# Side transfers behind weight loads, and lighter side work, in a hybrid encoder layer

## The chip, the cores and the metric

The kernel runs on one core of a Trainium2 chip. The time is the device time of one execution in microseconds (us), from runs of the whole kernel; a profile is one execution recorded by the hardware profiler. TensorE (PE) multiplies, VectorE (DVE), ScalarE (ACT) and GpSimd (POOL) do elementwise work, and SyncE (SP) sends nearly every transfer of this kernel.

## The reference

One layer of a bidirectional encoder on 1280 token rows of 2048 features: 1024 of a sample sequence and 256 of a prompt sequence.

```python
hn = rms_norm(x, norm_g)
xbc, z_ssd, dt_raw, q, k, v, z_att, mq, z_mem = split_cols(hn @ w_in, IN_SIZES)
xbc = silu(centred_dwconv(xbc, conv_w, conv_b))          # 1536 columns, 5 taps
xs, Bm, Cm = split_cols(xbc, (1024, 256, 256))
y = ssd_scan(forward) + ssd_scan(backward) + d_skip * xs  # 16 heads of 64, chunks of 128
o_ssd = rms_norm(y * silu(z_ssd), ssd_norm_g)            # in two groups
o_att = window_attention(q, k, v, sink) * silu(z_att)    # 8 heads, window 128
mk, mv = split_cols(rms_norm(mem, mem_norm_g) @ w_mem_kv, (512, 512))
o_mem = softmax(mq . mk) mv * silu(z_mem)                # 4 heads over 256 memory rows
return x + concat(o_ssd, o_att, o_mem) @ w_out
```

All of it is in float32.

## The kernel before, in words

**Products.** Each float32 operand is split into a high part (h, H) and a low part (l, L), and three TensorE products stand for one. A weight tile `wraw` (128 x 512) comes by a transfer, ScalarE makes `wh` of it (L211), VectorE `wl` (L212): that is `wsplit`. Its two instructions are kept in `marks`.

The tokens are two groups of 640 rows. `block_tok` is a plain block: sixteen weight tiles, and for each of them five token tiles (four for the memory rows) with three matmuls each, 512 or 288 columns (L266 to L268). Its last two weight tiles are used together, so that one token tile after another is finished and read out (`evac`). `block_pair` is the other kind, a seven-product (Strassen) form: 256 output columns are a unit, a unit has eight weight tiles with 21 matmuls of 320 columns each (L1155 to L1157), and for each weight tile GpSimd makes sums `ws` (L1127) that ScalarE and VectorE split into `sh` and `sl` as well. `weight_sums` sends the load of a pair weight tile two steps ahead (`lead=2`).

**Stages, in order of time.** Two memory blocks (`mk`, `mv`); the q block of the first group; the first pair stage, ten units of the first group; the kv and mq blocks of the first group; the second pair stage, ten units of the second group; then a mixed stage of plain blocks (kv, q, mq, z0, z1 of the second group, z0, z1 of the first, and the output blocks) between whose weight steps attention, memory attention and the scan are run; last eight output pair units.

**Side work of the first stages.** `x_stats` squares rows of x in pieces of 512 columns on ScalarE, to get a row factor in `rx`; `x_rows(grp)` turns five such factors into a row vector `rbc` over the group's 640 tokens with small TensorE products and copies on VectorE (L1461, L1462). `scale_row` multiplies a row tile of the turned x (`x_turned`, 128 features by 640 tokens) by the gain and `rbc` (L1186). For the first group `p_first` loads such a row pair, `p_fill` scales and splits it into the resident tiles `xH`, `xL`, `p_sums` and `p_split` make the pair sums. For the second group the rows are scaled in the first pair stage: `first_side` squares rows 5 to 9 in pieces of 320 columns (`square_tasks`), runs `x_rows(1)`, then loads, scales and stores each of sixteen rows in two halves to `xs_d` in DRAM (`row_tasks`, 32 tasks). In the kv and mq blocks `t_step` follows a plan `t_plan`: `p_next` loads a row pair from `xs_d`, `p_sums` and `p_split` make the pair sums from it in place, and later `r_load` and `r_fill` load the row again and make `xH` and `xL` of it. `keep_x` stores the first group's `xH` and `xL` to DRAM, 16 transfers of 640 KB, since the first group comes back late in the mixed stage.

The side steps are taken by `pairs_in`: after each weight step of a unit it calls `next(side)` zero to two times (eight times a unit).

**Order.** The program is written in one order, and a scheduler makes each engine's queue of it, taking what is ready first by its own reckoning. `tc.issue_after(ins)` queues what is traced in its block behind `ins`, and it does so for instructions of the same engine as `ins` only. `behind()` and `step()` open it for the two instructions in `marks` (ScalarE and VectorE). `block_tok` has a parameter `spaced`, which opens it around `wsplit` for a matmul two weight tiles back.

**Lanes.** In the mixed stage two lanes hold generators: lane 0 the windowed and the memory attention (`k_prep`, `attn`, `mem_attn`), lane 1 the scan (`ssd_up`, `ssd_down`). Each `yield` ends a step. After each weight step `pump(rates)` runs so many steps of each lane as `RATES` says for the block. So a yield between two operations puts TensorE's weight products between them.

Of the kernel before, what the change touches and what calls it, by code (L numbers as in the profile page):

```python
# [21 lines left out]
KT = D // P  # L22
# [6 lines left out]
CH, WB, RB, WA, WBB = 4, 3, 4, 5, 4  # L29
RBB = 3  # L30

RATES = {'kv': (1.8, 2.4), 'q': (2.95, 3.25), 'mq': (2.95, 3.25), 'z1': (2.95, 3.25), 'z0': (2.95, 3.25), 'oa': (2.4, 4.5), 'o': (4.2, 3.4)}
FAR = 1e30
# [8 lines left out]
def hymba_encoder_kernel(  # L42
# [139 lines left out]
    def fill_direct(q, j, src, gain=None, n=640, norm=False):  # L182
# [24 lines left out]
    count, middle = [0], {}  # L207

# [6 lines left out]
    def w_laid(src, n):  # L215

        def load(k, raw):
            S.dma_start(raw, src[k])
        return load, n
# [18 lines left out]

    def block_tok(w, nt, evac, before_last=None, feats=range(KT), places=range(KT), spaced=False):

# [4 lines left out]
        for k in range(last + 1):  # L245
            raw = wp.tile([P, 512], F32, tag="wraw", name="wraw", bufs=RB)
            load(feats[k], raw[:, :n])
            with tc.high_priority(offset=HP[2]):
                h = wp.tile([P, 512], F32R, tag="wh", name="wh", bufs=WB)
                l = wp.tile([P, 512], F32R, tag="wl", name="wl", bufs=WB)  # L250
                with tc.issue_after(middle[count[0] - 2]) if spaced and count[0] - 2 in middle else ExitStack():
                    wsplit(raw[:, :n], h[:, :n], l[:, :n])
            count[0] += 1
            hls[k] = h, l
            if k == last - 1:
                continue
            if k == last and before_last is not None:
                before_last(k)

            for t in range(nt):  # L260
                for k_ in ((k - 1, k) if k == last else (k,)):
                    q, m = divmod(places[k_], 4)
                    h, l = hls[k_]
                    sh = cur["H", q][:, m, t * P:(t + 1) * P]
                    sl = cur["L", q][:, m, t * P:(t + 1) * P]
                    T.matmul(ps[t][:, :n], sh, h[:, :n], start=(k_ == 0), stop=False)  # L266
                    T.matmul(ps[t][:, :n], sh, l[:, :n], start=False, stop=False)  # L267
                    mm = T.matmul(ps[t][:, :n], sl, h[:, :n], start=False, stop=(k_ == last))  # L268
                if k < last and t == nt // 2:
                    middle[count[0] - 1] = mm.ins  # L270
                elif k == last and t in (1, 3):
                    middle[count[0] - 2 + t // 2] = mm.ins
# [158 lines left out]
    def k_prep(t):  # L431
# [20 lines left out]
        yield  # L452
        yield
        ps = psum("pk")
        kf = kh.rearrange("p a b d -> p (a b d)")
# [93 lines left out]
    def attn(t):  # L549
# [24 lines left out]
        for b in range(2):  # L574
# [3 lines left out]
            V.tensor_sub(qh[:, :, 1, :], qb, qh[:, :, 0, :].bitcast(F32))  # L578
            yield
            ps = psum("pq")  # L580
            qf = qh.rearrange("p a b d -> p (a b d)")
# [81 lines left out]
    def mem_attn(t):  # L663
# [77 lines left out]
        yield  # L741
        yield
        turn_(0)
        yield
        turn_(1)
        yield
        values(0)
# [9 lines left out]
    def ssd_up(t):  # L757
# [63 lines left out]
        for g in range(2):  # L821
# [14 lines left out]
            if not last:  # L836
                fl = wb("fl", F32R)
                V.tensor_sub(fl, xf, fh.bitcast(F32))
            if not first:
                xb = wb("xb")  # L840
# [269 lines left out]
    def weight_sums(src, i):  # L1110
# [7 lines left out]
        else:  # L1118
            raw = wp.tile([P, 512], F32, tag="wraw", name="wraw", bufs=RB)
        S.dma_start(raw, src[i // 8, i % 8])  # L1120
        with tc.high_priority(offset=HP[2]):
# [109 lines left out]
    def p_next(k):  # L1231
        p_load(k, lambda r: xs_d[r])

# [19 lines left out]
    for k in range(8):  # L1253
        at = (4, 7, 10, 13, 15, 17, 19, 21)[k]
        for j, f in ((at - 3, p_next), (at, p_sums), (at + 2, p_split)):
            t_plan.setdefault(j, []).append((f, k))
    for k, at in enumerate((25, 26, 27, 28, 29, 31, 33, 35)):
        for j, f in ((at - 2, r_load), (at, r_fill)):
            t_plan.setdefault(j, []).append((f, k))

    def t_step(j):
        with ExitStack() as st:
            for ins in marks:
                st.enter_context(tc.issue_after(ins))
            if j in (27, 29):
                weight_sums(w_in_pairs, (j - 27) // 2)
            for f, k in sorted(t_plan.get(j, ()), key=lambda x: ((p_split, r_fill, p_sums, p_next, r_load).index(x[0]), x[1])):
                f(k)
# [271 lines left out]
    for _ in first[0]():  # L1540
# [8 lines left out]

    run(block_tok(w_in_rows("q"), 5, ev_raw(q_d, 0), feats=PAIRED, places=PAIRED), (0, 0),  # L1550
        extra=lambda k: p_step(16 + k))
# [6 lines left out]
    def pairs_in(grp, extra, side):  # L1558
        nonlocal owe
        for u, unit in enumerate(units):  # L1560
            for k in block_pair(w_in_pairs, u, rows_in, ev_seven(*unit, grp), lead=2):
                for _ in range((0 if k == 7 else 2 if k in (1, 4) else 1) if grp == 0 else k in (0, 1, 2, 4, 5)):
                    next(side, None)
# [6 lines left out]
                if u == 0:  # L1570
                    extra(32 + k)
                elif grp == 0 and keep and k in (1, 3, 5):
                    keep_x(*keep.pop(0))

    side = first_side()
    pairs_in(0, p_step, side)
# [42 lines left out]
    def tok(name, i, evac, after=None, extra=None, hold=0):  # L1619
        run(block_tok(w_in_rows(name), 5, evac, spaced=True), RATES[name], after, extra=extra, hold=hold)  # L1620

# [56 lines left out]
    for c, part_ in ((0, 0), (1, 0), (0, 1), (1, 1)):  # L1678
        h = halves[part_]
        run(block_tok(w_out_rows(c), 5, ev_out(c, part_), feats=h, places=h, spaced=True), RATES["o" if part_ else "oa"], hold=-1,  # L1680
            extra=late_rows(c, part_))
    for c in (2, 3):
        j0 = 16 * c - 48
        for k in block_tok(w_out_rows(c), 5, ev_out(c), before_last=lambda _: beside_step(j0 + 14), spaced=j0 < -16):
            if j0 + k == -7:
# [89 lines left out]
```

## Time and profile before

| what | value |
|---|---|
| median of 3 runs | 1830.43 us (1821.97 to 1832.84) |
| the profiled execution | 1830.21 us, its span 1828.5 us |
| mean granted TensorE clock | 0.995 |
| instructions | 31223, of which 10306 matmuls |
| TensorE busy | 1780.6 us (97%) |
| VectorE, ScalarE, GpSimd busy | 1332.2 (73%), 952.7 (52%), 682.1 (37%) |
| HBM read and written | 255.53 MB and 76.61 MB, 182 GB/s over the span |

A row of the table of stretches gives the stretch and its length, then for each engine its busy us and in brackets its instructions, then the granted TensorE clock as a share of full speed, the mean busy share of the sixteen DMA engines, and GB/s. A row of groups gives the source line, engine, operation, output and inputs, shapes and count, then busy us and mean ns of one, then the idle time just ahead of them and what ended it. A row of the timeline gives start and length in us, engine, line and operation, and in square brackets the idle time ahead of it. A row of waits gives who waited for whom, us in total, times, and the longest. A row of transfers ends with KB each and the median us from issue to landing. Matmuls overlap, so a count of them over a stretch says more of the pace than their durations. PE is TensorE's matmuls, PEld its weight loads.

### The profile page before, as it was taken

How to read it: one execution, taken by the hardware profiler on the slowest of the kernel's cores; microseconds unless marked ns; L12 is line 12 of the kernel's file. 1: busy time of each engine (PE TensorE's matmuls, PEld its weight loads, DVE VectorE, ACT ScalarE, POOL GpSimd, SP SyncE). 2: the span in 40 equal slices, each digit the busy share in tenths (PEclk: the TensorE clock that was granted, in tenths of full speed). 3: DMA queues.
4: the chain of work that ended last, by engine and by line, in shares of the span. 5: the costliest groups of instructions: out<-in, count | busy, mean ns of one | idle time of the engine just before them, and what ended most of it. 6: DMA issues, size and time to landing. Idle time of an engine off the chain costs nothing.

```text
span 1828.5 us, 31223 instructions
## 1 busy us (share of the span) xinstructions
PE 1780.6 (97%) x10306; PEld 1573.9 (86%) x10306; DVE 1332.2 (73%) x2489; ACT 952.7 (52%) x2135; POOL 682.1 (37%) x1092
## 2 busy tenths in 40 slices
PE   9999999999999999999999999999999999999999
PEld 7788998889799999987778877887777787889999
DVE  5594787997867889886667767767787865666665
ACT  6554553333555544366567447656556744443332
POOL 0115787871068899511001110001111100048775
PEclk9999999999999999999999999999999999999999
DMA  8685554665754443374545577657688765644442
GB/s 292 206 314 198 153 153 142 188 190 150 255 171 123 143 119 109 99 216 131 178 133 152 170 237 262 209 175 215 221 282 256 241 207 155 204 152 145 144 135 85
DMA packets 224674, 334.21 MB, mean 183 GB/s; under 512 B 23104, under 2 KB 102144, under 8 KB 224512
## 3 DMA queue, kind: packets, MB, share of 16 engines
q1 hardware_dynamic: 224368, 332.17, 58.8%
q8 instruction: 81, 1.33, 0.3%
q14 instruction: 81, 0.66, 0.1%
q10 hardware_dynamic: 144, 0.06, 0.0%
HBM read 255.53 MB, written 76.61 MB: 182 GB/s over the span
## 4 chain that ended last, share of the span: by engine, by line
PE 64%; DMA 12%; issue 7%; DVE 7%; POOL 6%; ACT 3%; SPq 1%; POOLq 0%; DVEq 0%; ACTq 0%
PE acc L266 8%; PE acc L267 8%; PE acc L268 7%; PE acc L1157 7%; PE acc L1155 7%; PE acc L1156 7%; POOL ws L1127 3%; PE accm L1155 3%; PE accm L1156 3%; PE accm L1157 3%; PE py L887 2%; DMA wraw<-in_w_in_pairs_dram 1%; DVE wl L212 1%; POOL wraw L1127 1%; PE pmo L733 1%
## 5 line engine op out<-in xcount | busy, mean ns | idle before, releaser
L266 PE MATMUL acc<-wh,xH 128*128 128x512 f32 (+1 forms) x1248 | 483.7, 388 | 2.7 <-ACT wh L211 1.7
L267 PE MATMUL acc<-wl,xH 128*128 128x512 f32 (+1 forms) x1248 | 478.3, 383 | 4.2 <-DVE wl L212 4.1
L268 PE MATMUL acc<-wh,xL 128*128 128x512 f32 (+1 forms) x1248 | 475.5, 381 | 0.0
L212 DVE TENSOR_TENSOR wl<-wraw,wh 128x512 fp32r<-128x512 f32 (+1 forms) x480 | 350.9, 734 | 152.2 <-ACT wh L211 149.0
L211 ACT ACTIVATE wh<-wraw 128x512 fp32r<-128x512 f32 (+1 forms) x480 | 290.2, 611 | 195.7 <-PE acc L268 117.1
L211 ACT ACTIVATE sh<-ws 128x384 fp32r<-128x384 f32 x224 | 116.7, 524 | 337.1 <-POOL ws L1127 179.3
L267 PEld LDWEIGHTS acc<-wl,xH 128*128 128x128 f32 x1248 | 235.8, 189 | 49.7 <-DVE wl L212 9.0
L1127 POOL TENSOR_TENSOR ws<-wraw 128x128 f32<-128x128 f32 x224 | 152.5, 681 | 337.2 <-DMA wraw<-in_w_in_pairs_dram 194.0
L266 PEld LDWEIGHTS acc<-wh,xH 128*128 128x128 f32 x1248 | 235.6, 189 | 48.0 <-ACT wh L211 3.6
L268 PEld LDWEIGHTS acc<-wh,xL 128*128 128x128 f32 x1248 | 235.6, 189 | 41.8 <-issue 0.7
L212 DVE TENSOR_TENSOR sl<-ws,sh 128x384 fp32r<-128x384 f32 x224 | 156.7, 702 | 128.3 <-ACT sh L211 125.5
L1127 POOL TENSOR_TENSOR ws<-wraw,ws 128x128 f32<-128x128 f32 x224 | 150.3, 671 | 17.6
L1127 POOL TENSOR_TENSOR ws<-ws,wraw 128x128 f32<-128x128 f32 x224 | 149.3, 667 | 0.0
L1127 POOL TENSOR_TENSOR wraw<-wraw 128x128 f32<-128x128 f32 x224 | 139.5, 623 | 17.6
L595 POOL COPY lg<-nsink 128x2 f32<-128x2 f32 x40 | 17.7, 443 | 267.5 <-PE ppt L623 144.5
L1157 PE MATMUL acc<-xH,wl 128*128 128x320 f32 x320 | 100.1, 313 | 7.7 <-DVE wl L212 7.7
L1155 PE MATMUL acc<-tH,sh 128*128 128x320 f32 x320 | 99.9, 312 | 1.1 <-ACT qs L291 1.0
L1157 PE MATMUL acc<-tH,sl 128*128 128x320 f32 x320 | 99.5, 311 | 0.0
L1156 PE MATMUL acc<-tL,sh 128*128 128x320 f32 x320 | 99.5, 311 | 0.0
L1155 PE MATMUL accm<-tH,wh 128*128 128x320 f32 x320 | 99.1, 310 | 0.3 <-DVE u L1305 0.2
L1155 PE MATMUL acc<-xH,wh 128*128 128x320 f32 x320 | 99.4, 311 | 0.0
L1156 PE MATMUL acc<-xL,wh 128*128 128x320 f32 x320 | 99.0, 309 | 0.0
(473 smaller groups left out, 3944.6 us busy)
## 6 DMA issues: line engine op xcount, KB each, us to landing
wraw<-in_w_in_pairs_dram SPq DMA_DIRECT2D x160, 256.0 KB, 2.8
wraw<-in_w_in_laid_dram SPq DMA_DIRECT2D x128, 256.0 KB, 3.5
wraw<-in_w_out_laid_dram SPq DMA_DIRECT2D x64, 256.0 KB, 3.5
wraw<-in_w_out_pairs_dram SPq DMA_DIRECT2D x64, 256.0 KB, 2.8
xH<-xH SPq DMA_DIRECT2D x16, 640.0 KB, 5.9
xL<-xL SPq DMA_DIRECT2D x16, 640.0 KB, 6.3
rf<-ac SPq DMA_DIRECT2D x40, 256.0 KB, 4.2
rb<-ac SPq DMA_DIRECT2D x40, 256.0 KB, 4.4
```

The costliest lines, as they stand in the source:

```text
L211: a = A.activation(h, raw, AF.Copy)
L212: b = V.tensor_sub(l, raw, h.bitcast(F32))
L266: T.matmul(ps[t][:, :n], sh, h[:, :n], start=(k_ == 0), stop=False)
L267: T.matmul(ps[t][:, :n], sh, l[:, :n], start=False, stop=False)
L268: mm = T.matmul(ps[t][:, :n], sl, h[:, :n], start=False, stop=(k_ == last))
L595: G.tensor_copy(lg[:, :, nk:nk + 1], ns8[:, rr, :].unsqueeze(2))
L733: T.matmul(po[:, j * P:(j + 1) * P], mv[:, a, h * P:(h + 1) * P], pT[:, (2 * j + a) * P:(2 * j + a + 1) * P], start=(a == 0), stop=(a == 1))
L887: T.matmul(py[:, h * 64:h * 64 + 64], mt[:, (h % 4) * P:(h % 4 + 1) * P], xsT[g][:, h * 64:h * 64 + 64], start=True, stop=True)
L1127: G.tensor_tensor(out=o, in0=x, in1=y, op=op)
L1155: T.matmul(ps[p], h, xh, start=(k_ == 0), stop=False)
L1156: T.matmul(ps[p], h, xl, start=False, stop=False)
L1157: T.matmul(ps[p], l, xh, start=False, stop=(k_ == 7))
```

## The change

- The load of every weight tile is kept in `fetched`, and `behind()` (side tasks, `keep_x`) and the steps of `x_stats` are queued behind it too; as it is on SyncE, this holds for their transfers.
- The squares of the second group's rows (5 to 9) are done by `x_stats` in lane 0 beside the q block, at 1.6 steps per weight step, and leave `first_side`, which begins with three empty steps.
- `row_tasks` scales rows k and k+8 for k below `SCALED` = 5, ten rows. The other six are loaded from `x_turned` in the kv and mq blocks, scaled by the new `p_scale` and stored to `xs_d`; the plan's last three row pairs move by one to three steps, and the refills' first five by one.
- `pairs_in` takes a side step after weight steps 1, 3 and 5 of a unit, and keeps rows after 2 and 4.
- `spaced`, with `count` and `middle`, is taken out.
- Yields are added in `k_prep`, `attn` (two), `mem_attn` (three) and, for the first tiles of the two sequences, `ssd_up`; `RATES` change with them.

```diff
+SCALED = 5
-RATES = {..., 'q': (2.95, 3.25), 'mq': (2.95, 3.25), 'z1': (2.95, 3.25), 'z0': (2.95, 3.25), 'oa': (2.4, 4.5), 'o': (4.2, 3.4)}
+RATES = {..., 'q': (3.45, 3.3), 'mq': (3.45, 3.3), 'z1': (3.45, 3.3), 'z0': (3.45, 3.3), 'oa': (3.1, 4.4), 'o': (4.1, 3.4)}
...  step()
-                for ins in marks:
+                for ins in marks + (fetched if name[0] == "x_stats" else []):
...
+    fetched = []
+
     def behind():
         st = ExitStack()
-        for ins in marks:
+        for ins in marks + fetched:
...  w_laid(), and the same in weight_sums()
-            S.dma_start(raw, src[k])
+            fetched[:] = S.dma_start(raw, src[k]).ins,
...  block_tok()
-                with tc.issue_after(middle[count[0] - 2]) if spaced and count[0] - 2 in middle else ExitStack():
-                    wsplit(raw[:, :n], h[:, :n], l[:, :n])
+                wsplit(raw[:, :n], h[:, :n], l[:, :n])
...  k_prep(), after the split of kh; attn(), after each split of qh
+        yield
...  mem_attn(), after the load of mq; after scores(1); after turn_(1)
+        yield
...  ssd_up(), after fl
+                if first:
+                    yield
...
     def p_next(k):
-        p_load(k, lambda r: xs_d[r])
+        p_load(k, (lambda r: xs_d[r]) if k < SCALED else (lambda r: x_row(1, r)))
+
+    def p_scale(k):
+        for i, x in enumerate(raw[k]):
+            scale_row(k + 8 * i, x)
+            S.dma_start(xs_d[k + 8 * i], x)
...  t_plan
-        at = (4, 7, 10, 13, 15, 17, 19, 21)[k]
-        for j, f in ((at - 3, p_next), (at, p_sums), (at + 2, p_split)):
+        at = (4, 7, 10, 13, 15, 18, 21, 24)[k]
+        if k < SCALED:
+            todo = (at - 3, p_next), (at, p_sums), (at + 2, p_split)
+        else:
+            todo = (at - 4, p_next), (at - 2, p_scale), (at, p_sums), (at + 1, p_split)
+        for j, f in todo:
...
-    for k, at in enumerate((25, 26, 27, 28, 29, 31, 33, 35)):
+    for k, at in enumerate((26, 27, 28, 29, 30, 31, 33, 35)):
...
-    def x_stats(_):
-        yield from stats([(xrow(t), t) for t in range(5)],
+    def x_stats(grp):
+        yield from stats([(xrow(t), t) for t in range(5 * grp, 5 * grp + 5)],
...  row_tasks()
-        for r in range(KT):
+        for r in [k + 8 * i for k in range(SCALED) for i in range(2)]:
...  first_side()
-        yield from side_work(square_tasks([(xrow(t), t) for t in range(5, 10)]))
+        for _ in range(3):
+            yield
...
-    run(block_tok(w_in_rows("q"), 5, ...), (0, 0),
+    queue(0, x_stats, [1])
+    run(block_tok(w_in_rows("q"), 5, ...), (1.6, 0),
...  pairs_in()
-                for _ in range((0 if k == 7 else 2 if k in (1, 4) else 1) if grp == 0 else k in (0, 1, 2, 4, 5)):
+                if k in ((1, 3, 5) if grp == 0 else (0, 1, 2, 4, 5)):
                     next(side, None)
...
-                elif grp == 0 and keep and k in (1, 3, 5):
+                elif grp == 0 and keep and k in (2, 4):
                     keep_x(*keep.pop(0))
```

More of the change, by code (lines that the diff above doesn't have):

```diff
@@ L199, in fill_direct @@
         yield
+    fetched = []
     def behind():
         st = ExitStack()
-        for ins in marks:
+        for ins in marks + fetched:
             st.enter_context(tc.issue_after(ins))
         return st
-    count, middle = [0], {}
     def wsplit(raw, h, l):
@@ L237, in hymba_encoder_kernel, with block_tok @@
     PAIRED = [k + 8 * i for k in range(8) for i in range(2)]
-    def block_tok(w, nt, evac, before_last=None, feats=range(KT), places=range(KT), spaced=False):
+    def block_tok(w, nt, evac, before_last=None, feats=range(KT), places=range(KT)):
         load, n = w
@@ L267, in block_tok @@
                     T.matmul(ps[t][:, :n], sh, l[:, :n], start=False, stop=False)
[L268 to L272, printed above, removed]
+                    T.matmul(ps[t][:, :n], sl, h[:, :n], start=False, stop=(k_ == last))
                 if k == last:
@@ L745, in mem_attn @@
         turn_(1)
+        yield
         yield
@@ L838, in ssd_up @@
                 V.tensor_sub(fl, xf, fh.bitcast(F32))
+                if first:
+                    yield
             if not first:
@@ L1119, in weight_sums @@
             raw = wp.tile([P, 512], F32, tag="wraw", name="wraw", bufs=RB)
-        S.dma_start(raw, src[i // 8, i % 8])
+        fetched[:] = S.dma_start(raw, src[i // 8, i % 8]).ins,
         with tc.high_priority(offset=HP[2]):
@@ L1266, in t_step @@
                 weight_sums(w_in_pairs, (j - 27) // 2)
-            for f, k in sorted(t_plan.get(j, ()), key=lambda x: ((p_split, r_fill, p_sums, p_next, r_load).index(x[0]), x[1])):
+            for f, k in sorted(t_plan.get(j, ()), key=lambda x: ((p_split, r_fill, p_sums, p_scale, p_next, r_load).index(x[0]), x[1])):
                 f(k)
@@ L1414, in first_side @@
     def first_side():
-        yield from side_work(square_tasks([(xrow(t), t) for t in range(5, 10)]))
+        for _ in range(3):
+            yield
         for _ in x_rows(1):
@@ L1548, in hymba_encoder_kernel @@
     run(block_tok(w_mem_rows(1), 4, ev_mv, places=TURNED), MR[1], extra=p_step)
-    run(block_tok(w_in_rows("q"), 5, ev_raw(q_d, 0), feats=PAIRED, places=PAIRED), (0, 0),
+    queue(0, x_stats, [1])
+    run(block_tok(w_in_rows("q"), 5, ev_raw(q_d, 0), feats=PAIRED, places=PAIRED), (1.6, 0),
         extra=lambda k: p_step(16 + k))
@@ L1571, in pairs_in @@
                     extra(32 + k)
-                elif grp == 0 and keep and k in (1, 3, 5):
+                elif grp == 0 and keep and k in (2, 4):
                     keep_x(*keep.pop(0))
+    assert not lanes[0]
     side = first_side()
@@ L1619, in tok @@
     def tok(name, i, evac, after=None, extra=None, hold=0):
-        run(block_tok(w_in_rows(name), 5, evac, spaced=True), RATES[name], after, extra=extra, hold=hold)
+        run(block_tok(w_in_rows(name), 5, evac), RATES[name], after, extra=extra, hold=hold)
     queue(1, vectors, [0])
@@ L1679, in hymba_encoder_kernel @@
         h = halves[part_]
-        run(block_tok(w_out_rows(c), 5, ev_out(c, part_), feats=h, places=h, spaced=True), RATES["o" if part_ else "oa"], hold=-1,
+        run(block_tok(w_out_rows(c), 5, ev_out(c, part_), feats=h, places=h), RATES["o" if part_ else "oa"], hold=-1,
             extra=late_rows(c, part_))
@@ L1683, in hymba_encoder_kernel @@
         j0 = 16 * c - 48
-        for k in block_tok(w_out_rows(c), 5, ev_out(c), before_last=lambda _: beside_step(j0 + 14), spaced=j0 < -16):
+        for k in block_tok(w_out_rows(c), 5, ev_out(c), before_last=lambda _: beside_step(j0 + 14)):
             if j0 + k == -7:
```

3 lines of the change are left out of this document (1 added, 2 removed).

## The prediction

> **What bounds the kernel now.** I read the page first, then a table of busy time by stage with stretches cut where the kind of TensorE work changes, then the waits, the timeline and the transfers inside the stretches that lose time.
>
> ```profile
> PE 1780.6 (97%) x10306; PEld 1573.9 (86%) x10306; DVE 1332.2 (73%) x2489; ACT 952.7 (52%) x2135; POOL 682.1 (37%) x1092
> ```
> ```profile
> core 0: us, PE busy (x) PEld busy (x) DVE busy (x) ACT busy (x) POOL busy (x), PEclk, DMA share, GB/s
> 5.00:98.00 93.00, 91.75 (x399) 73.49 (x398) 51.56 (x85) 54.57 (x108) 6.11 (x14) 1.00 0.79 258
> 98.00:158.00 60.00, 56.96 (x244) 46.19 (x243) 44.06 (x73) 26.84 (x46) 12.63 (x20) 0.97 0.82 295
> 158.00:272.00 114.00, 112.53 (x763) 111.51 (x762) 81.11 (x129) 64.17 (x156) 89.55 (x142) 1.00 0.52 150
> 272.00:290.00 18.00, 14.62 (x82) 14.23 (x82) 11.86 (x20) 4.51 (x9) 13.51 (x22) 0.81 0.25 77
> 290.00:426.00 136.00, 127.70 (x849) 124.26 (x848) 119.67 (x184) 55.45 (x100) 102.31 (x143) 1.00 0.59 178
> 460.00:516.00 56.00, 54.95 (x241) 44.51 (x242) 41.20 (x69) 29.70 (x51) 13.28 (x20) 1.00 0.81 260
> 516.00:763.00 247.00, 246.37 (x1680) 246.03 (x1680) 201.90 (x325) 121.45 (x254) 202.32 (x305) 1.00 0.41 123
> 763.00:1627.00 864.00, 840.92 (x4467) 681.31 (x4465) 622.02 (x1352) 502.73 (x1247) 97.45 (x178) 1.00 0.64 198
> 1550.00:1600.00 50.00, 50.00 (x222) 41.40 (x222) 35.55 (x64) 24.17 (x41) 0.00 (x0) 1.00 0.65 199
> 145.10:149.00 3.90, 0.88 (x3) 0.19 (x1) 2.75 (x5) 2.54 (x6) 2.88 (x5) 1.00 0.21 54
> 149.00:152.40 3.40, 3.38 (x7) 2.33 (x8) 2.06 (x4) 0.59 (x1) 0.21 (x1) 0.50 0.58 208
> 282.20:288.90 6.70, 6.02 (x23) 6.05 (x24) 2.38 (x6) 0.52 (x1) 3.32 (x8) 0.50 0.14 42
> 1398.30:1401.70 3.40, 3.40 (x11) 2.73 (x10) 3.36 (x6) 2.15 (x4) 0.00 (x0) 0.50 1.02 325
> 1514.40:1517.70 3.30, 3.30 (x11) 2.72 (x12) 1.38 (x2) 1.15 (x2) 1.22 (x2) 0.50 0.40 122
> ```
>
> TensorE bounds it, so only time in which its stream stalls or its clock is halved can be won. Two undisturbed stretches give prices. The second pair stage, 516 to 763, does 1680 matmuls of 320 columns in 247 us: 0.147 each. The plain block at 1550 does 222 of 512 columns in 50 us: 0.225 each. Held against these, the q block's end (145 to 152) has 3 matmuls in 3.9 us (3.2 lost) and then 3.4 us at a clock of 0.50 (1.7 lost): 4.9. From 272 to 290, 82 x 0.147 = 12.1 of 18 us, of which ten small matmuls explain about 1: 4.9 lost. From 290 to 426, 849 x 0.147 = 124.8 of 136: 11.2 lost. From 158 to 272, 763 x 0.147 = 112.2 of 114: nothing worth having. The mq block, 460 to 516, loses about 2, the second pair stage nothing. The mixed stage from 763 loses in many small waits.
>
> **The q block's end: kept rows leave it.** In the code `keep_x` stands in the pair units; the trace shows where its sixteen stores run.
>
> ```profile
> L1467 SPq DMA_DIRECT2D xH<-xH x8: 320/428/1374, 86.8 to 149.4; - x8
> L1467 SPq DMA_DIRECT2D xL<-xL x8: 326/426/840, 88.9 to 151.8; - x8
> ```
> ```profile
> wraw<-in_w_in_pairs_dram SPq DMA_DIRECT2D x5, 256.0 KB, 5.2
> ```
> ```profile
> 143.67 0.46 POOL L1127 TENSOR_TENSOR ws<-wraw 128x128 f32<-128x128 f32 x1 [29.35 <-DMA wraw<-in_w_in_pairs_dram]
> ```
> ```profile
> 145.66 0.52 ACT L211 ACTIVATE sh<-ws 128x384 fp32r<-128x384 f32 x1 [7.44 <-POOL ws L1127]
> ```
> ```profile
> 147.21 0.51 PE L266 MATMUL acc<-wh,xH 128*128 128x512 f32 x1 [1.73 <-ACT wh L211]
> ```
>
> They start between 86.8 and 151.8, before the first pair unit: `behind()` held back only ScalarE and VectorE, and SyncE sent the stores as soon as the rows were made. They share the block with the first pair weights, which take 5.2 us to land against 2.8 over the whole run (below). GpSimd gets them late, ScalarE stands 7.44 us at the sums' split, which is queued ahead of the q block's last weight split, and TensorE starves. With `fetched` the stores queue behind a pair weight load and cannot run here: 16 x 640 KB, 10.5 MB, leave. I take the whole 4.9 (bounds 0 and 4.9).
>
> **What enters the q block.** Twenty loads of 256 KB (5.2 MB) with twenty squares, in 512-column pieces.
>
> ```profile
> L1346 ACT ACTIVATE xst<-xst 128x512 f32<-128x512 f32 x20 | 12.5, 626 | 10.2 <-DMA xst<-in_x_sample_dram 10.2
> L1346 ACT ACTIVATION_READ_ACCUMULATOR xst<-xst 128x1 f32 x20 | 3.7, 186 | 0.0
> ```
>
> ScalarE gains 16.2 us on 26.8 of 60: covered. The block's traffic falls on balance, 10.5 MB out and 5.2 in. The risk is a square that waits for its piece ahead of a weight split: the first group's twenty waited 10.2 us in the mem blocks, and that stretch (399 x 0.225 = 89.8 of 93) lost 3.2 for all reasons. Bounds 0 and +10.2; I take +1. Ordering the first group's loads behind weights too is in the same bounds.
>
> **The first pair stage.** Squares leave it (35 loads, no VectorE work to speak of); they ran from 158 to 272, where nothing is lost, so that is worth 0. Twelve of 32 half-row scalings leave, and the other twenty go at three steps a unit in place of eight.
>
> ```profile
> L1186 DVE SCALAR_TENSOR_TENSOR xrow<-xrow,vec,rbc 128x320 f32<-128x320 f32 x32 | 20.4, 640 | 9.6 <-DMA xrow<-in_x_turned_dram 6.4 <-issue 2.4 <-DVE wl L212 0.6
> ```
> ```profile
> PE acc L1157 <- DVE wl L212: 7.5, 5, 2.5
> ```
> ```profile
> 700.00:750.00 50.00, 50.00 (x343) 50.00 (x342) 45.62 (x72) 23.80 (x42) 44.67 (x64) 1.00 0.36 114
> 300.00:310.00 10.00, 10.00 (x71) 10.00 (x70) 7.63 (x12) 4.11 (x7) 8.12 (x14) 1.00 0.81 256
> ```
> ```profile
> wraw<-in_w_in_pairs_dram SPq DMA_DIRECT2D x160, 256.0 KB, 2.8
> ```
>
> All 32 scalings lie in 290 to 426, 20.4 us of VectorE in a stretch that had 119.7 of 136 busy; TensorE's waits there are for VectorE's `wl`, 7.5 us. At TensorE's own pace (124.8 us) the demand is 96%. Without the scalings it is 99.3 of 124.8, 80%; three a unit of 24.7 us add 1.9, 8 points: 88%. The second pair stage held full pace at 45.62 of 50, 91%. So most of the loss goes: I take -9 of 11.2 (bounds 0 and -11.2).
>
> `x_rows(1)` moves from the fifth unit to the second, in the same form: two transposed sums, the second of which waits for VectorE's copy of the first.
>
> ```profile
> 282.88 0.77 PE L1461 MATMUL prx<-identr,rx 128*128 128x128 f32 x2 [3.38 <-DVE rbc L1462]
> ```
>
> That wait, 3.38, and the half clock after it (6.7 us at 0.50) are the 4.9. In the second unit VectorE has gates left over rather than two conv tiles, so the copy is nearer: I take -3 (bounds -4.9 and 0). The Trainium skill (TensorE: Matmul & The Clock Gate, What's actually happening) says that about 3.4 us of idling halves the clock; 3.38 here did, agreeing. By that rule a wait just under it would save the 3.35 alone and the sum would hardly move.
>
> The sixteen kept rows now run here, two a unit, behind a weight load. Bounds: 0, and 16 x (5.2 - 2.8) = +38 if every following weight load lands as late as in the q block and TensorE waits for it. The stage has room: at 300 the transfers ran at 256 GB/s beside a full TensorE. I take +1, nearer that row. The Trainium skill (DMA: Bandwidth & Descriptors, Two DMAs through the same engine are not ordered) says that descriptors of one queue start in order, so a weight load behind 640 KB waits; no run here shows the cost alone. By that rule the term would be the +38 without slack, and the sum positive; it is the fifth rival.
>
> **The kv and mq blocks.** Six rows are loaded unscaled, scaled and stored there.
>
> ```profile
> L1186 DVE SCALAR_TENSOR_TENSOR ra<-ra,vec,rbc 128x640 f32<-128x640 f32 x8 | 7.0, 880 | 0.0
> ```
> ```profile
> 100.00:110.00 10.00, 10.00 (x46) 8.29 (x45) 9.96 (x16) 5.53 (x10) 0.64 (x1) 1.00 0.97 344
> ```
>
> Six scalings of 0.88 are 5.3 us on VectorE's 41.2 of 56. Six stores add 2.0 MB to 14.6: 296 GB/s, below the 344 seen at 100. The sums overwrite the row that the store reads, two steps later (2 x 15 x 0.225 = 6.8 us, against landings of 2.8 for transfers of like size). If that cover went, three late stores of 2.8 and the 5.3 would be +14. Bounds 0 and +14, taken +2. The stores also stand on SyncE until VectorE has scaled, ahead of weight loads: in the same bound. The second pair stage keeps its work: 0.
>
> **The mixed stage.** `spaced` ordered weight splits behind a matmul, but an order binds instructions of the same engine, and the split has none on TensorE: removing it costs 0 and brings 0. The added yields stand exactly before waits of the trace.
>
> ```profile
> PE pst L817 <- DVE fl L838: 3.9, 2, 2.6
> PE pmq L679 <- DMA mq<-mq: 3.4, 1, 3.4
> PE pmt L718 <- DVE mpr L710: 2.2, 2, 1.6
> PE pst L816 <- ACT fh L830: 2.0, 2, 1.3
> PE ppt L623 <- DVE nm L603: 1.8, 2, 0.9
> PE pk L457 <- ACT kh L449: 1.6, 2, 1.0
> PE pq L583 <- DVE qh L578: 1.3, 1, 1.3
> ```
>
> The state yield is for the first tiles alone, and of the 5.9 us at `pst` the two longest waits, 2.6 and 1.3, are theirs: 3.9. With pmq 3.4, pmt 2.2, pk 1.6, pq 1.3 that is 12.4; the two stretches at half clock (1398 and 1514) add (3.4 + 3.3)/2 = 3.4: 15.8 in reach. One step is not always enough (pmq waits 3.4, a step is under 2), so half: -8. Against it, the first lane runs 3.45 steps per weight step in place of 2.95, and what has no new yield comes sooner: +1. Taken -7; bounds -15.8 and +35 (rival below). By a count of yields, lane 0 has 504 steps in place of 444, and its rates hand out 505 in place of 448: no heap is left at the drain.
>
> **Sum.** -4.9 + 1 - 9 - 3 + 1 + 2 - 7 = -19.9. The profiled execution took 1830.2 (span 1828.5); its time is the median of the runs shown, 1830.4, within 0.2. Forecast: 1830.2 - 19.9 = 1810.3, said as 1810.
>
> **Rivals.** First, lanes gain nothing and the second sum waits as before: -4.9 + 1 - 9 + 1 + 2 = -9.9, 1820. For it: the waits in the mixed stage are scattered, and moving steps moves them. Against: six of the seven rows above have a yield of their own. Second, the squares in the q block land late and ScalarE holds the splits, +10.2 in place of +1, with lanes neutral: 1820.3 + 9.2 - 3 = 1826. For it: 10.2 in the mem blocks; against: the block's traffic falls. Third, slower: the squeezed lane. In 800 to 1550 about 137 weight steps take 750 us, 5.5 each; a lane step falls from 5.5/2.95 = 1.86 to 5.5/3.45 = 1.59, 0.27 less. Attention's ten entries to TensorE without a new yield (four scores, four turns, two values) in ten tiles and three in ten mem tiles are 130; at no slack they cost 130 x 0.27 = 35. Then 1830.2 - 12.9 + 35 = 1852. It decides once idle time before the score, turn and value matmuls grows by more than 13 us. For it: ppt waits already (1.8); against: such waits are few today. Fourth, the stores stay early despite `fetched`, because the order names a load that itself goes early: without -4.9 and with the rows' gain, 1815, inside the forecast's range. Fifth, weight loads behind the kept rows' stores in the pair stage land 2.4 late sixteen times and TensorE waits for each: +38 in place of +1, 1847. For it: 5.2 against 2.8 when both run; against: the row at 300.
>
> **How the numbers follow.** Forecast 0.56 (the fourth rival with it), first rival 0.18, second 0.07, third 0.16, fifth 0.03. The forecast's own range is 1790 (all of 15.8, 11.2 and 4.9 twice, near -37, and a little more) to 1818; the range goes to 1838 to hold the first two rivals and the mild part of the third. A change of about 1% is what a measurement of this kernel can tell from none (1812.1 and 1848.7): faster 0.56, same 0.28, slower 0.16.
>
> **What would show it.** Right: the sixteen stores start after 160; no wait of GpSimd and ScalarE before 150; 290 to 426 at 0.147 a matmul with VectorE under 92%; pmq, pmt and pst waits halved; the second pair stage still 247. Wrong: first pair stage still above 260 us; ScalarE waiting for `xst` in the q block by over 5 us; TensorE's idle time in the mixed stage above today's.

## The result, and the profile after

The changed kernel takes 1823.62 us (median of 20 runs, 1817.36 to 1830.93) against 1830.12 (20 runs): a ratio of 0.9968, 95% interval 0.9954 to 0.9982, so 6.5 us or 0.3% less. The profiled execution took 1827.17 us, 3.6 above its own median, so stage differences of a few us are read with care.

The stages below go from the first matmul of one to the first of the next, in us, one profiled execution each; the differences are of the unrounded times. The forecast column holds the prediction's terms.

| stage | before | after | difference | forecast |
|---|---|---|---|---|
| memory blocks and q block | 152.1 | 152.6 | +0.5 | -3.9 |
| first pair stage | 268.3 | 252.9 | -15.4 | -11 |
| kv and mq blocks | 89.4 | 96.5 | +7.2 | +2 |
| second pair stage | 247.4 | 248.5 | +1.1 | 0 |
| mixed stage | 864.5 | 868.8 | +4.2 | -7 |
| last units | 201.5 | 201.1 | -0.4 | 0 |

The page of the changed kernel has the same picture of its engines as before:

```profile
PE 1779.1 (97%) x10306; PEld 1571.8 (86%) x10306; DVE 1336.6 (73%) x2483; ACT 949.3 (52%) x2105; POOL 679.8 (37%) x1092
```

Its table of busy time by stretch (q block, first pair stage, mq block, second pair stage, mixed stage; the last two rows are the end of the q block):

```profile
core 0: us, PE busy (x) PEld busy (x) DVE busy (x) ACT busy (x) POOL busy (x), PEclk, DMA share, GB/s
97.70:158.00 60.30, 57.50 (x240) 46.50 (x239) 44.67 (x77) 38.13 (x84) 16.73 (x30) 0.94 0.68 226
158.00:411.00 253.00, 249.49 (x1693) 247.63 (x1692) 211.63 (x314) 110.40 (x198) 198.86 (x296) 1.00 0.55 174
444.00:507.50 63.50, 58.57 (x243) 45.90 (x243) 48.63 (x79) 30.77 (x53) 13.82 (x20) 0.97 0.82 260
507.50:756.00 248.50, 247.07 (x1682) 246.45 (x1682) 202.81 (x325) 121.37 (x253) 201.78 (x304) 1.00 0.43 124
756.00:1625.00 869.00, 842.88 (x4472) 680.99 (x4471) 621.26 (x1354) 502.93 (x1250) 97.98 (x178) 1.00 0.64 197
...
144.40:148.00 3.60, 1.85 (x6) 0.67 (x4) 3.52 (x9) 2.75 (x7) 1.39 (x2) 1.00 0.16 18
148.00:154.80 6.80, 5.75 (x14) 4.49 (x15) 1.66 (x4) 1.20 (x2) 4.61 (x10) 0.50 0.38 130
```

The first pair stage now does 1693 matmuls in 253.0 us, 0.149 each, at full clock. The q block's traffic fell from 295 to 226 GB/s, as the stores left it, and yet its end stalls as before: 6 matmuls of 0.225 are 1.35 of 3.6 us, and 14 are 3.15 of 6.8 at a clock of 0.50, so 5.9 us are lost where 4.9 were. The transfers did move. The changed kernel's transfers by line, first to last start in us:

```profile
L1479 SPq DMA_DIRECT2D xH<-xH x8: 422/424/430, 178.1 to 340.3; - x8
L1479 SPq DMA_DIRECT2D xL<-xL x8: 423/426/488, 202.8 to 366.9; - x8
```

What ScalarE does in that time (its timeline at the end of the q block, nothing left out) names another cause:

```profile
140.51 0.53 ACT L212 ACTIVATE sh<-ws 128x384 fp32r<-128x384 f32 x1 [2.93 <-POOL ws L1129]
140.95 0.72 ACT L1226 ACTIVATE tH<-ra 128x640 fp32r<-128x640 f32 x1
143.21 0.53 ACT L212 ACTIVATE sh<-ws 128x384 fp32r<-128x384 f32 x1 [1.54 <-POOL ws L1129]
143.64 0.72 ACT L1226 ACTIVATE tH<-rb__1345 128x640 fp32r<-128x640 f32 x1
144.27 1.13 ACT L212 ACTIVATE wh<-wraw 128x512 fp32r<-128x512 f32 x2
```

The plain block's last weight splits, `wh` at 144.27, stand in ScalarE's queue behind two splits of the next stage's pair sums, `sh`. Those wait 2.93 and 1.54 us for GpSimd, and TensorE then waits for the weights. The mq block, which lost 2 us before, loses more by the same order, shown on ScalarE and, in the second fence, on TensorE:

```profile
497.28 0.52 ACT L212 ACTIVATE sh<-ws 128x384 fp32r<-128x384 f32 x1 [5.67 <-POOL ws L1129]
497.71 0.45 ACT L1401 ACTIVATE sst<-sst 128x320 f32<-128x320 f32 x1
498.07 0.19 ACT L1401 ACTIVATION_READ_ACCUMULATOR sst<-sst 128x1 f32 x1
498.16 0.61 ACT L212 ACTIVATE wh<-wraw 128x512 fp32r<-128x512 f32 x1
```
```profile
498.83 0.50 PE L265 MATMUL acc<-wh,xH 128*128 128x512 f32 x1 [3.67 <-ACT wh L212]
```

This order isn't new: in the kernel before, the mq block's last two `wh` stood behind an `sh` as well. What is new is how long that `sh` waits, 5.67 us in place of 2.71:

```profile
504.54 0.53 ACT L211 ACTIVATE sh<-ws 128x384 fp32r<-128x384 f32 x1 [2.71 <-POOL ws L1127]
...
505.43 0.61 ACT L211 ACTIVATE wh<-wraw 128x512 fp32r<-128x512 f32 x1
```

GpSimd starts that sum later, measured against TensorE. Before, it starts at 501.87, 5.7 us ahead of the matmuls of the block's last two weight tiles (507.6); now it starts at 495.32, 1.0 us behind them (494.3):

```profile
501.87 1.15 POOL L1127 TENSOR_TENSOR ws<-wraw 128x128 f32<-128x128 f32 x1 [23.81 <-DMA wraw<-in_w_in_pairs_dram]
```
```profile
495.32 0.45 POOL L1129 TENSOR_TENSOR ws<-wraw 128x128 f32<-128x128 f32 x1 [31.77 <-DMA ra<-xs]
```

The five loads of pair weights beside the mq block take 5.8 us to land (median), against 3.9 before.

### The profile page after: what moved, and what is told of

Read it like the earlier page. It is cut to its first block, busy times and chain, and to the rows that moved or that the text cites. A ratio compares the mean times of both kernels' runs of the same rounds, so it can differ in the third digit from the quotient of the medians.

```text
span 1825.5 us, 31108 instructions
## 1 busy us (share of the span) xinstructions
PE 1779.1 (97%) x10306; PEld 1571.8 (86%) x10306; DVE 1336.6 (73%) x2483; ACT 949.3 (52%) x2105; POOL 679.8 (37%) x1092
## 4 chain that ended last, share of the span: by engine, by line
PE 70%; DMA 12%; DVE 8%; ACT 4%; issue 3%; POOL 2%; SPq 1%; DVEq 0%; ACTq 0%; POOLq 0%
PE acc L266 9%; PE acc L267 9%; PE acc L265 8%; PE acc L1159 8%; PE acc L1157 8%; PE acc L1158 8%; PE accm L1158 3%; PE accm L1157 3%; PE accm L1159 3%; PE py L889 2%; DVE wl L213 2%; PE po L630 1%; DMA wraw<-in_w_in_laid_dram 1%; PE ppt L620 1%; DMA wraw<-in_w_in_pairs_dram 1%
## 5 line engine op out<-in xcount | busy, mean ns | idle before, releaser
L213 DVE TENSOR_TENSOR wl<-wraw,wh 128x512 fp32r<-128x512 f32 (+1 forms) x480 | 351.6, 735 | 144.4 <-ACT wh L212 139.8
L1129 POOL TENSOR_TENSOR ws<-wraw 128x128 f32<-128x128 f32 x224 | 143.0, 639 | 271.8 <-DMA wraw<-in_w_in_pairs_dram 91.5
L1129 POOL TENSOR_TENSOR ws<-ws,wraw 128x128 f32<-128x128 f32 x224 | 153.8, 687 | 0.0
L1159 PE MATMUL accm<-tH,wl 128*128 128x320 f32 x320 | 98.9, 309 | 0.0
## 6 DMA issues: line engine op xcount, KB each, us to landing
wraw<-in_w_in_pairs_dram SPq DMA_DIRECT2D x160, 256.0 KB, 2.7
wraw<-in_w_in_laid_dram SPq DMA_DIRECT2D x128, 256.0 KB, 3.6
wraw<-in_w_out_laid_dram SPq DMA_DIRECT2D x64, 256.0 KB, 4.0
wraw<-in_w_out_pairs_dram SPq DMA_DIRECT2D x64, 256.0 KB, 2.8
rf<-ac SPq DMA_DIRECT2D x40, 256.0 KB, 4.1
rb<-ac SPq DMA_DIRECT2D x40, 256.0 KB, 4.2
```

The source lines that it names most:

```text
L213: b = V.tensor_sub(l, raw, h.bitcast(F32))
L1129: G.tensor_tensor(out=o, in0=x, in1=y, op=op)
L1159: T.matmul(ps[p], l, xh, start=False, stop=(k_ == 7))
```

## The experiments

Each group of runs shared a chip and the runs of the kernel before. The chips differ (the kernel before took 1831.4, 1827.1, 1824.4 and 1829.0 us on the four), so kernels are compared within a group. Stage times are of one profiled execution, as above; for kernels that differ only in the lanes, the first pair stage comes out within 2 us. A stall at the end of the q block varies more: the same block takes 59.7 us in the kernel before and 57.0 in the second run, 60.7 in the change and 62.0 in the first run, in part by how long the clock is halved behind the stall.

**First group: the parts alone, and another queue order.** The first run takes the lanes' part out of the change: `RATES` and yields as before.

> The changed kernel with the yields and RATES of before in the mixed stage. Squeezed-lane theory (the new yields remove 10 us of waits but scores, turns and values come sooner and cost more): the mixed stage falls from 869 back to about 864 us, the time to about 1819. Rival (the lanes brought the forecast 7 us and the profile's mixed stage is chance): the time rises to about 1830.

Measured: 1826.42, ratio 0.9968 (0.9955 to 0.9980), the ratio of the whole change.

The second gives the kernel before the new lanes alone.

```diff
-RATES = {'kv': (1.8, 2.4), 'q': (2.95, 3.25), ...}
+RATES = {'kv': (1.8, 2.4), 'q': (3.45, 3.3), ...}
...
+        yield    # the six places of the change
```

> The kernel before with the new yields and RATES alone. Squeezed-lane theory: 1834, with longer waits before the score and turn matmuls and shorter ones at pst, pmq, pk, pq. Rival (lanes gain 7): 1823.

Measured: 1831.88, ratio 1.0011 (0.9999 to 1.0022). The lanes gain nothing that these intervals show, added or taken out.

The third takes `fetched` out of the order, so that stores and loads of the side work go as soon as SyncE can send them.

```diff
...  step()
-                for ins in marks + (fetched if name[0] == "x_stats" else []):
+                for ins in marks:
...  behind()
-        for ins in marks + fetched:
+        for ins in marks:
```

> The changed kernel with side transfers queued behind the weight splits only, as before, so the kept rows' stores run in the q block again, now beside the squares' loads. Queue-order theory (the stall at the q block's end comes from the sums' split standing ahead of the last weight splits on ScalarE, whatever the traffic): the q block's end stalls about as long as with the change, the time is 1823 to 1826. Traffic theory (my forecast: the stores make the pair weights late): the q block grows by 5 us or more, the time is about 1829.

Measured: 1822.17, ratio 0.9955 (0.9943 to 0.9967): no slower than the change, though the q block's traffic is back (the q block of this kernel):

```profile
97.40:158.70 61.30, 57.20 (x242) 45.98 (x241) 45.25 (x78) 38.54 (x83) 19.93 (x30) 0.97 0.88 302
```

The block takes 61.2 us at 302 GB/s and 60.7 at 226: it stalls with the stores and without, and the difference is smaller than that between two profiles of the same block.

The fourth moves no work. It queues the first two pair weights' splits of a pair stage behind the plain block's last split (in `block_pair`).

```diff
-                wsplit(raw, h[0], l[0])
-                wsplit(sums, h[1], l[1])
+                with ExitStack() as st:
+                    if u == 0 and k < 2:
+                        for ins in marks:
+                            st.enter_context(tc.issue_after(ins))
+                    wsplit(raw, h[0], l[0])
+                    wsplit(sums, h[1], l[1])
```

> The changed kernel with the splits of the first two pair tiles of each pair stage queued behind the plain block's last weight split on ScalarE and VectorE. Queue-order theory: the stalls at the ends of the q block (about 5 us with the half clock) and of the mq block (about 6 us) go, and the time falls to about 1813. Traffic theory: the last weight splits wait for their own transfers, and the time stays at 1822 to 1824.

Measured: 1809.87, ratio 0.9882 (0.9869 to 0.9894), 16.6 us below the first run of the group. Its q and mq blocks, and ScalarE at the end of the mq block:

```profile
94.40:148.80 54.40, 54.40 (x242) 45.05 (x241) 45.95 (x77) 37.51 (x83) 19.59 (x27) 1.00 0.76 253
432.40:489.50 57.10, 55.99 (x240) 44.78 (x241) 47.34 (x73) 30.10 (x52) 10.44 (x13) 1.00 0.84 272
```
```profile
480.11 1.14 ACT L212 ACTIVATE wh<-wraw 128x512 fp32r<-128x512 f32 x2
481.15 0.92 ACT L212 ACTIVATE sh<-ws 128x384 fp32r<-128x384 f32 x2
```

Now `wh` stands ahead of `sh`. The q block does 242 matmuls in 54.4 us, 0.225 each: nothing is lost. Memory blocks 91.9 to 89.0, q block 60.7 to 54.4, mq block 63.6 to 57.1: 15.7 us from one order. In the memory blocks of the changed kernel an `sh` had stood ahead of three reads of finished tiles (`mkr`), in the kernel before likewise:

```profile
48.85 0.53 ACT L212 ACTIVATE sh<-ws 128x384 fp32r<-128x384 f32 x1 [3.65 <-POOL ws L1129]
49.28 1.55 ACT L362 ACTIVATE mkr<-acc 128x512 f32<-128x512 f32 x3
```

**Second group: the split order beneath parts of the change.** The kernel before with the split order:

> The kernel before with the split order of the fourth run alone (the splits of the first two pair tiles queued behind the plain block's last weight split). Queue-order theory: the memory blocks fall from 92 to 89 us and the q block from 60 to 55, although the kept rows' stores still run there; the mq block, which had no stall, stays at 57: about 1823, ratio 0.9955. Traffic theory: the q block keeps its loss, about 1829, ratio 0.999.

Measured: 1819.01, ratio 0.9952 (0.9934 to 0.9969). Its q block and first pair stage:

```profile
94.40:148.80 54.40, 54.40 (x242) 45.06 (x241) 46.54 (x72) 26.73 (x47) 16.37 (x20) 1.00 0.93 330
148.80:414.20 265.40, 256.38 (x1691) 254.45 (x1690) 216.01 (x333) 124.15 (x266) 204.82 (x307) 0.97 0.54 160
```

With thirteen of the sixteen stores sent in it, at 330 GB/s, the q block loses nothing. The cause named in the prediction falls with this row. The memory blocks fall from 92.3 to 89.1, most of the 3.2 us that the prediction read as lost there.

The change with the split order and the old lanes:

> The changed kernel with the split order and with the old yields and RATES. If the lanes are worth nothing, as the first two runs say, the ratio is that of the fourth run, 0.988, within 0.0015. If they gain the 7 us of the forecast, 0.992; if they cost 4, 0.986.

Measured: 1808.07, ratio 0.9882 (0.9859 to 0.9905). Against the run above, the change without its lanes is worth 10.9 us once the order is mended in both. The first pair stage falls by 12.6 (265.4 to 252.8), and the second gives 3.0 back (248.1 to 251.1): at its start TensorE waits 2.4 us for ScalarE's reads of the mq block, against 1.1, and the clock is then halved for 3.4 us.

The change with the split order and without `fetched` in the order:

> The changed kernel with the split order and with side transfers queued as before, so that the kept rows' stores run in the q block beside the squares' loads. Queue-order theory: the q block stays within 1 us of 54.4, ratio 0.988. Traffic theory: with 5 MB more than before in that block the weights come late and it grows by 5 us or more, ratio 0.991 or more.

Measured: 1809.55, ratio 0.9896 (0.9874 to 0.9918), the same as with it. Its sixteen stores run early, and its q block still has full pace with stores and squares in it together:

```profile
L1483 SPq DMA_DIRECT2D xH<-xH x8: 423/424/697, 83.7 to 164.5; - x8
L1483 SPq DMA_DIRECT2D xL<-xL x8: 425/587/1307, 85.8 to 170.6; - x8
```
```profile
94.60:149.00 54.40, 54.40 (x241) 45.06 (x241) 43.86 (x72) 37.24 (x81) 17.26 (x24) 1.00 0.90 314
```

How late the pair weights land doesn't decide the stall either. In this q block they take 6.0 us, more than the 5.2 of the kernel before, and nothing is lost; in the changed kernel's they take 2.6, and it stalls (this run first, then the change):

```profile
wraw<-in_w_in_pairs_dram SPq DMA_DIRECT2D x5, 256.0 KB, 6.0
```
```profile
wraw<-in_w_in_pairs_dram SPq DMA_DIRECT2D x5, 256.0 KB, 2.6
```

The change with the split order and the old pace of the side steps, eight a unit:

```diff
-                if k in ((1, 3, 5) if grp == 0 else (0, 1, 2, 4, 5)):
+                for _ in range((0 if k == 7 else 2 if k in (1, 4) else 1) if grp == 0 else k in (0, 1, 2, 4, 5)):
```

> The changed kernel with the split order, and the side steps of the first pair stage taken eight times a unit as before in place of three; ten rows are scaled, as in the change. VectorE-demand theory (pace): the twenty scalings fall into some three units again, where demand passes 96%, and of the 11 us of the first pair stage about 7 come back: 259 us, ratio 0.992. Number theory (twelve tasks fewer are what counts): the stage stays within 2 us of 252, ratio 0.989.

Measured: 1816.83, ratio 0.9931 (0.9911 to 0.9950), 7 to 9 us above its neighbours. Its first pair stage, and TensorE's largest wait there:

```profile
148.80:400.60 251.80, 249.08 (x1691) 247.46 (x1690) 213.73 (x316) 111.96 (x200) 201.87 (x299) 1.00 0.54 175
```
```profile
149.90:408.00 258.10, 251.33 (x1691) 247.56 (x1690) 211.05 (x316) 111.57 (x200) 201.21 (x300) 1.00 0.52 171
```
```profile
PE acc L1163 <- DVE wl L213: 5.6, 6, 1.5
```

The first fence is the new pace (the fourth run), the second the old. Work and counts are equal and VectorE is busy 211 of 258: only the pace of the side steps differs, and it costs 4 to 6 us here (the three kernels with the new pace so far take 251.9, 252.8 and 253.9).

**Third group: how many rows, when, and one lane alone,** all with the split order. All sixteen rows scaled in the first stage again, at four steps a unit:

```diff
-SCALED = 5
+SCALED = 8
-                if k in ((1, 3, 5) if grp == 0 else (0, 1, 2, 4, 5)):
+                if k in ((1, 3, 4, 5) if grp == 0 else (0, 1, 2, 4, 5)):
```

> The split order, with all sixteen rows scaled in the first pair stage at four even side steps a unit (32 half-row tasks, none in the mq block). Pace theory: even spread keeps VectorE's demand near 90% and the stage stays within 3 us of 252, ratio 0.988 to 0.990. Number theory: twelve more scalings cost the stage 5 us or more, ratio 0.991 or above. The mq block, at 57 us with the scaling in it, can win 1 us at most.

Measured: 1809.88, ratio 0.9916 (0.9900 to 0.9932). The first pair stage takes 256.0 us, 2 to 4 more than with ten rows:

```profile
149.00:404.90 255.90, 249.96 (x1691) 247.44 (x1690) 220.47 (x328) 111.21 (x200) 201.89 (x299) 1.00 0.57 188
```

The kv and mq blocks take 87.5 against 88.9 of the fourth run: by these rows, six rows moved win 1 to 3 us in all.

The old pace with `x_rows(1)` in the fifth unit, by 37 empty steps ahead of it in place of 3:

> The split order, the old side pace (eight steps a unit) and 37 empty steps ahead of x_rows(1), so that it stands in the fifth unit again and the twenty scalings follow at the old pace, with the squares still in the q block. If the second sum's wait for VectorE depends on the unit (conv tiles beside it), the wait of 3.4 us and the half clock come back and the first pair stage is 5 us above the 258 of the eighth run: about 263, ratio 0.996. If it went away for another reason, 258, ratio 0.993.

Measured: 1812.18, ratio 0.9926 (0.9907 to 0.9945); first pair stage 256.8, no worse than 258.1 of the eighth run. The second sum's wait:

```profile
269.19 0.46 PE L1477 MATMUL prx<-identr,rx 128*128 128x128 f32 x2 [1.30 <-DVE rbc L1478]
```

It waits 1.30 us and not the 3.38 of the kernel before: the unit alone does not bring that stall back.

The old lanes, and of the lanes' part only the scan's yield (`ssd_up`, first tiles, with 3.3 and 4.4 steps for its lane):

```diff
+                if first:
+                    yield
```

> The split order, the old yields and rates in lane 0, and in lane 1 the change's yield for the first tiles with its rates (3.3 and 4.4). Squeezed-lane theory: the scan's wait at pst falls from about 5 us to under 2 while score and turn waits stay at their old 2 to 4, so the mixed stage falls by 3 us or more: ratio 0.986. Rival (a removed wait is made up by whatever comes next on TensorE): 0.988.

Measured: 1804.95, ratio 0.9892 (0.9874 to 0.9911); mixed stage 858.3.

**Fourth group: three lanes on one chip,** all with the split order: the sixth, the eleventh and the fourth kernel again.

> The kernel of the sixth run again (split order, old yields and rates), on one chip with the next two. Reference for both.

> The kernel of the eleventh run again (the change's yield and rates in the scan lane alone). Squeezed-lane theory: below the old lanes by 4 us or more and its interval clear of theirs, with the mixed stage near 860. Rival (a removed wait is made up by what comes next): the same as the old lanes within 2 us, and the profile of 858 us was chance.

> The kernel of the fourth run again (all of the change's yields and rates). Squeezed-lane theory: above the scan lane alone by 4 us or more, within 2 us of the old lanes, with the waits of scores and turns at 10 us or more in all. Rival: all three the same.

Measured: old lanes 1810.77 (ratio 0.9899, 0.9877 to 0.9921), scan yield alone 1806.48 (0.9880, 0.9856 to 0.9903), new lanes 1810.56 (0.9895, 0.9872 to 0.9918). By means, old lanes less new are 0.6 ± 2.5 us, and old lanes less scan alone 3.6 ± 3.7: the first is nothing, the second leans to a gain that the interval doesn't quite show; new less scan alone is 3.0 ± 3.2. The mixed stage takes 867.9, 861.9 and 870.4 us in their profiles. Groups of TensorE's instructions in the mixed stage (busy us, mean ns | idle us just ahead), first of the old lanes, then of the new:

```profile
L618 PE MATMUL ppt<-identr,lg 128*128 128x128 f32 x208 | 32.3, 277 | 3.8 <-DVE nm L598 2.5 <-ACT pT L619 0.7 <-DVE lg L606 0.6
L596 PE MATMUL psc<-kT,qT 128*128 128x384 f32 (+1 forms) x80 | 27.8, 352 | 0.2
L812 PE MATMUL pst<-fl,bth 128*128 128x512 f32 x16 | 6.6, 411 | 3.4 <-DVE fl L833 3.4
L674 PE MATMUL pmq<-identr,mq 128*128 128x128 f32 x40 | 5.3, 258 | 3.8 <-DMA mq<-mq 3.8
```
```profile
L620 PE MATMUL ppt<-identr,lg 128*128 128x128 f32 x208 | 32.9, 282 | 7.8 <-ACT pT L621 2.8 <-ACT lg L604 2.7 <-DVE nm L600 2.3
L598 PE MATMUL psc<-kT,qT 128*128 128x384 f32 (+1 forms) x80 | 28.7, 365 | 3.9 <-ACT pT L621 2.4 <-DVE nm L600 0.9 <-ACT qT L582 0.3
L817 PE MATMUL pst<-fl,bth 128*128 128x512 f32 x16 | 6.3, 392 | 0.0
L677 PE MATMUL pmq<-identr,mq 128*128 128x128 f32 x40 | 4.8, 242 | 0.0
```

The wait at `pst` goes, 3.4 us, and `pmq`, 3.8 with the old lanes, waits for nothing with the new. Turns and scores (`ppt`, `psc`), which have no new yield, wait 7.7 us more (4.0 and 3.7). The idle time in the stage is 24.9 us with the old lanes and 24.4 with the new, summed over the groups, and 19.6 with the scan's yield alone.

## Why the prediction was right or wrong

**The q block's end: the step that failed.** The prediction blamed the kept rows' traffic for the stall. It quoted the right row, ScalarE standing 7.44 us at a split "queued ahead of the q block's last weight split", and took away the lateness, not the place in the queue. The runs show the place: with the stores gone the stall stays (5.9 us for 4.9), with stores and the split order it is gone (54.4 us at 330 GB/s). How late the pair weights land doesn't decide it by itself (6.0 us without loss, 2.6 with). The size, 4.9, was about right for the profile that it was read from: the order is worth 5.3 in that q block, and 2.6 in the same block of the second run, where the clock wasn't halved. It just wasn't in this change.

**The kv and mq blocks.** Forecast +2, measured +7.2, of which 6.3 are the mq block's. The moved rows' own work is about as forecast: with the split order the two blocks take 88.9 us with six rows scaled in them (fourth run) and 87.5 with none (fifth and ninth). The rest needs the order of `sh` ahead of `wh`, since it goes with the split order (57.1). That order stood in the kernel before too, and the prediction didn't name it there; with the change the sums come late enough for it to cost. All three profiles with the change's plan for these blocks and the old order show it (mq block 61.6 to 63.6), and neither of those with the old plan does (57.2 and 59.0). Which of the moved loads, scalings and stores makes the sums late stays open. The bound of +14, made for late transfers, held the loss.

**The mixed stage.** Forecast -7, and the lanes bring 0. The yields did what they were meant to at `pst` and `pmq`, which no longer wait, though at `pk` the wait stays at 1.8 us. But the third rival's mechanism was there at about 8 us, where the prediction took +1 and the rival 35; 8 won and 8 given back is the nothing of the first, second and fourteenth runs. That the stage took 868.8 in the profile of the change stays partly open: the first run, with old lanes, shows 868.8 too. Taking `spaced` out costs nothing, as forecast: the stage takes 866.5 us in the fifth run, which keeps it, and 866.2 in the sixth, which doesn't.

**What was right.** The first pair stage: -11 for its rows and the second sum, -15.4 measured. The pace accounts for 4 to 6 of it, by the eighth run. The other 7 to 10 us, between its 258 and the 265 to 268 of the kernels with the old side work, hold the six rows fewer (2 to 4 by the ninth run, which has a step a unit more as well), the second sum's wait and the squares' leaving, which the tenth run couldn't part. The second sum's stall, of which the prediction took 3 of 4.9, went whole: in the changed kernel it waits for nothing and the clock stays full through the stage. That the unit does it isn't shown; the prediction's zero for the squares' leaving isn't either. VectorE is busy 211.63 of 253.0, 84%, and TensorE's waits for `wl` fell from 7.5 us (the prediction's row) to 3.5:

```profile
PE acc L1159 <- DVE wl L213: 3.5, 5, 1.3
```

The squares in the q block cost nothing (54.4 with them and without). The kept rows' stores in the pair stage cost nothing: 251.9 with them, 253.9 without. The Trainium skill (DMA: Bandwidth & Descriptors, Two DMAs through the same engine are not ordered) says that descriptors of one queue start in order, from which the fifth rival made +38. No run speaks against that order, and its price here is 0. That the loads go two steps ahead may be why; no run takes that lead away. The changed kernel's pair weights land no later than before, 2.7 us against 2.8:

```profile
wraw<-in_w_in_pairs_dram SPq DMA_DIRECT2D x160, 256.0 KB, 2.7
```

The fourth rival's order (stores stay early) was made in the third and seventh runs, and it costs nothing: queueing the side transfers behind weight loads moves transfers and no time.

**Altogether.** Without the q block's 4.9 and the lanes' 7 the prediction's terms come to -8 (+1 - 9 - 3 + 1 + 2). The change without its lanes, measured with the split order on both sides, is -10.9. In the change itself 6.3 of that went to the mq block, where the old order met later sums.

## What to carry to other kernels

When an engine waits ahead of work that others need, ask first why the waiting instruction stands there: an instruction whose input comes from a third engine, placed early in a queue, stops what is ready behind it. Queueing it behind the block's last weight splits gave 16 us in the changed kernel, more than twice what the whole change did, and 8 in the kernel before. An order that costs little can begin to cost when an edit makes its input later, as in the mq block, so the ends of all blocks are compared after each. A yield in a lane with a raised rate takes its room from the lane's other steps; a gain at the named waits is counted only with the waits that it moves.

## What the hardware showed that was not expected

TensorE's clock halved without a long gap. In the changed kernel's q block the waits from 144.4 to 149.05 are short, the last of them the longest, 1.61 us, and from 148.0 to 154.8 the clock is 0.50:

```profile
146.47 0.50 PE L266 MATMUL acc<-wl,xH 128*128 128x512 f32 x1 [1.03 <-DVE wl L213]
...
149.05 0.79 PE L266 MATMUL acc<-wl,xH 128*128 128x512 f32 x1 [1.61 <-DVE wl L213]
```

A single wait of 2.5 us in the kernel before (the prediction's row for `wl`) lies in a stretch that kept 1.00. The Trainium skill (TensorE: Matmul & The Clock Gate, What's actually happening) puts the drop behind an idle window of some 3.4 us that runs freely; here a stretch of 3.6 us with 1.85 busy sufficed, so the longest gap alone doesn't tell. Nor does the busy share of a stretch: one of the same length with less busy time kept 1.00 in the second run (row below). Where the window lies may decide, but no run here shows it.

```profile
144.60:148.20 3.60, 1.57 (x6) 0.79 (x6) 3.56 (x6) 0.90 (x2) 2.24 (x4) 1.00 0.48 101
```

And transfers at 314 to 330 GB/s beside a TensorE at full pace cost it nothing.
